# Low parts of weight units in a two-layer trunk: an accumulating DMA in place of a VectorE subtraction

## The chip, the cores and the metric

The kernel runs on one core of a Trainium2 chip. The metric is the device time of one execution in microseconds; the time before is a median of three runs, 1868.06 us (1867.34 to 1868.14). PE is TensorE, DVE is VectorE, ACT is ScalarE, POOL is GpSimd, SP is SyncE, which issues the loads.

## What is computed

Two layers on a sequence of 512 tokens of width 1024, in float32. Each layer is a feed-forward, a mixer (windowed attention beside retention) and a second feed-forward, each followed by a layer norm. Cut to what matters:

```python
D_FF = 2816
def swiglu_ffn(x, w_gu, w_down):
    a, u = jnp.split(x @ w_gu, 2, axis=-1)
    return (jax.nn.silu(a) * u) @ w_down

for l in range(2):
    x = layer_norm(ALPHA * x + 0.5 * swiglu_ffn(x, ffn1_w_gu[l], ffn1_w_down[l]), ...)
    x = layer_norm(ALPHA * x + hybrid_mixer(x, w_in[l], w_out[l], ...), ...)
    x = layer_norm(ALPHA * x + 0.5 * swiglu_ffn(x, ffn2_w_gu[l], ffn2_w_down[l]), ...)
```

## The kernel before

Every large product is made of three products in a reduced-precision form of float32: each operand is split into a high part (the value rounded, by a cast on ACT) and a low part (the value minus the high part, by a subtraction on DVE). The method split (lines 151 to 156) does that, and mm3 (158 to 163) multiplies high by high, high by low and low by high into one PSUM bank. The lines 161, 162 and 163 of the profile are these three; nearly all of PE's work has them.

The weights come as a stream of units. A unit is 128 x 1024 values as a high tile uh and a low tile ul. The class Weights holds the units in the order of their use: load brings 1 MB from HBM into one of two raw buffers (enough for two units, or for the blocks of several), then a function called cut makes the unit from it. A unit lives in one of six pairs of slots (UBUFS); pump makes the next unit as soon as done has given one back, so the cast of a unit waits for PE's last product with the unit six places before it. A raw buffer is given back when the last cut has read it.

A feed-forward has two stages.

- The up stage makes 22 chunks of the hidden layer. Its first two pairs of chunks are made by plain products, the other nine pairs by Winograd's seven products of blocks (seven_items makes the units, seven and glu7 use them). For such a pair the stream has seven units: first (the blocks A11 | A12), s12 and s34 (sums S1 | S2 and S3 | S4 of the blocks, added on DVE into a tile S), last (A22 of the gate and of the up half), and again first, s12, s34 for the up half. Units of s12 are the first ones multiplied with the sums of the input, Th and Tl; first has xh and xl. S has two buffers.
- The down stage goes over the 22 chunks of the hidden layer: rows_item makes one unit of 128 rows of w_down for each chunk, and each unit meets eight products of three matmuls. The chunk itself is split on ACT and DVE into hh and hl (line 565). The units of the last four chunks (TAIL) have slots of their own, so pools is set for them. The norm follows: norm, lines 386 to 410, on DVE with one power on POOL, and then PE's transposes (line 370) of the normed rows back into xh and xl.

The mixer's output projection takes its eight units from rows_item as well: the first four, with heads set, into mixer buffers, the last four into the common slots. Line 872 is the power on POOL in the retention, line 401 that of the norm.

The order on each engine comes from a scheduler that fills the engines' queues ahead of time; each engine then takes its queue in order, waiting on semaphores.

Of the kernel before, what the change touches and what calls it, by code (L numbers as in the profile page):

```python
# [7 lines left out]
F32 = mybir.dt.float32  # L8
# [31 lines left out]
class Weights:  # L40
    """Units of weights in the order of their use: loaded, then split into hi + lo, ahead of it."""

# [28 lines left out]
    def take(self):  # L71
        """A pair of the slots of units for something else, until done()."""
        self.out += 1
        return self.T.units()
# [6 lines left out]
    def done(self, n=1):  # L81
        self.out -= n
        self.pump()


class Trunk:
# [20 lines left out]

    # The products run as one stream; whatever hangs on other engines' results is a task that
    # yields for a number of steps of that stream.
    def spawn(self, gen, delay=0):  # L110
# [40 lines left out]
    def split(self, hi, lo, src):  # L151
        a = self.nc.scalar.copy(hi, src)  # L152
        b = self.nc.vector.tensor_sub(lo, src, hi.bitcast(F32))  # L153
        if self.pin:
            self.tc.keep_in_program_order(a)
            self.tc.keep_in_program_order(b)

    def mm3(self, out, a, b, start, stop):
        (ah, al), (bh, bl) = a, b
        mm = self.nc.tensor.matmul  # L160
        mm(out, ah, bh, start=start, stop=False)  # L161
        mm(out, ah, bl, start=False, stop=False)  # L162
        mm(out, al, bh, start=False, stop=stop)  # L163
# [5 lines left out]

# [1 line left out]
    def cols_item(self, w, c0, key):  # L171
        """Two units of 128 columns each, all rows."""
        def load():
            v = self.raw().rearrange("p (k c) -> p k c", k=KC)
            src = w[:, c0 : c0 + 256].rearrange("(k p) c -> p k c", p=P)
            if self.later is not None:
                self.later.append(lambda: self.nc.sync.dma_start(v[:, :, P:], src[:, :, P:]))
                self.nc.sync.dma_start(v[:, :, :P], src[:, :, :P])
            else:
                self.nc.sync.dma_start(v, src)  # L180
            return v

        def cut(c):
            def go(v, hi, lo):
                hv, lv = (t.rearrange("p (k c) -> p k c", k=KC) for t in (hi, lo))
                self.split(hv, lv, v[:, :, c * P : (c + 1) * P])
                return hv, lv
            return go

        return [(key, load, None, cut(c)) for c in range(2)]  # L190

    def pair_item(self, w, c0, key):
        """The same, with the columns of each head sorted into even and odd ones."""
        load = self.cols_item(w, c0, key)[0][1]
# [12 lines left out]
    def heads_item(self, w, cp, key):  # L207
        """Query heads: unit c holds head c and head 4 + c."""
        def load():
# [15 lines left out]
    def wide_item(self, w, c0, kh, key):  # L225
        """Two units of two row chunks each, 512 columns."""
        def load():
# [13 lines left out]
    def rows_item(self, w, r0, key, pools, heads=False):  # L241
        """Two units of 128 rows each, all 1024 columns; with heads, in the order of the query units."""
        def load():
# [10 lines left out]
        def cut(c):  # L254
            def go(v, hi, lo):
                self.split(hi, lo, v[:, c, :])
                return hi, lo
            return go
# [3 lines left out]
    def seven_items(self, a, u):  # L262
        """Units for the seven-product form of two pairs of column chunks: the blocks of the weights
        A11 | A12, the sums S1 | S2 and S3 | S4 of each pair, and A22 of both."""
        sums = {}
# [13 lines left out]
        def s12(q):  # L279
            def go(v, hi, lo):  # L280
                s = sums[q] = self.gpool.tile([P, 4, KC // 2, P], F32, tag="S", name=self.nm("S"), bufs=2)
                a11, a12, a21, a22 = blocks(v)
                self.nc.vector.tensor_add(s[:, 0], a21, a22)
                self.nc.vector.tensor_sub(s[:, 1], s[:, 0], a11)
                hv, lv = wide(hi), wide(lo)
                self.split(hv, lv, s[:, 0:2].rearrange("p s k c -> p (s k) c"))
                return hv, lv
            return go
# [52 lines left out]

# [1 line left out]
    def proj(self, out, u, t0, t1):  # L343
# [20 lines left out]
    def to_xT(self, src, t, c0, dst=None):  # L364
        """Transposes four 128-column chunks of token group t and splits them."""
        nc = self.nc
# [44 lines left out]

# [1 line left out]
    def tail_units(self):  # L413
        return self.units(self.fpool, "tl", TAIL)

    def ffn(self, g, b, out=None):
        nc, tc, W = self.nc, self.tc, self.W
        with ExitStack() as ctx:
# [8 lines left out]
            def sums_of_x():  # L427
                """T1 = B12 - B11, T2 = B22 - T1, T3 = B22 - B12 and -T4 = B21 - T2, split."""
                x = hT[:, NF - KC :, :]
# [26 lines left out]
            def seven(u0, getu, q, u22):  # L456
                """Winograd's form: seven products of blocks for a pair of chunks."""
                w, x, y, z = (self.ps() for _ in range(4))
# [136 lines left out]

# [1 line left out]
    def big(self, shape, dt=F32):  # L597
# [310 lines left out]
def tables():  # L908
    """Constants of the shapes alone: rotations, masks and decays."""
    import numpy as np  # L910
# [55 lines left out]
```

## Time and profile before

| | |
|---|---|
| runs, median of three | 1868.06 us (1867.34 to 1868.14) |
| profiled execution, first to last instruction (span) | 1864.8 us |
| what the runs' median has beyond that span | 3.3 us |
| granted PE clock over the span | 0.999 |
| PE, weight loads on PE, DVE, ACT, POOL busy | 99%, 91%, 72%, 43%, 5% |
| DMA: share of the 16 engines' time in loads | 30.0% |
| loads of 1 MB, median from issue to landing | 4.7 to 5.1 us |

The profiled execution has no time of its own beside its span; the runs are timed without the profiler. In a row of groups stand the line, the engine, the operation, what it writes and reads, how many of them, busy time in all and the mean in ns, and then the idle time before them with what ended it. In the list of waits stand the waiting instruction, whom it waited for, the sum in us, how often, and the longest. In a timeline stand start and length in us.

### The profile page before, as it was taken

To read this page: it belongs to the slowest core of one execution; us is meant where nothing else is said; L and a number is where in the kernel's file an instruction comes from. 1 tells how busy PE (TensorE), PEld (TensorE's weight loads), DVE (VectorE), ACT (ScalarE), POOL (GpSimd) and SP (SyncE) were. 2 spreads that over 40 slices of the span, in tenths; PEclk is the share of its full clock that TensorE was granted. 3 is DMA by queue.
4 is the path that set the end of the run, shared out by engine and by line. 5 is a ranking of instruction groups with operands and counts; after the bars stand their busy time and mean duration, and the time that the engine had idled before them with its cause. 6 is when DMAs were issued, how large, how long until landed. Compare 5 with 4: busy or idle time off the path is not lost.

```text
span 1864.8 us, 29046 instructions
## 1 busy us (share of the span) xinstructions
PE 1848.5 (99%) x12180; PEld 1691.5 (91%) x12180; DVE 1349.2 (72%) x1861; ACT 792.7 (43%) x1212; POOL 88.1 (5%) x80
## 2 busy tenths in 40 slices
PE   8999999999999999999999999999999999999998
PEld 8999988888889999998899999889888899999886
DVE  7889844657857799963688998447578577999535
ACT  5444433278622444443234444332785234444330
POOL 0000000110210000000000000002002100000001
PEclk9999999999999999999999999999999999999999
DMA  5233244122312232243212323441224122233421
GB/s 181 91 104 124 91 155 139 63 80 69 91 69 68 83 122 91 94 156 131 96 46 96 109 91 114 138 156 41 80 69 113 46 91 91 91 114 114 136 90 45
DMA packets 136930, 184.87 MB, mean 99 GB/s; under 512 B 3936, under 2 KB 115296, under 8 KB 136800
## 3 DMA queue, kind: packets, MB, share of 16 engines
q1 hardware_dynamic: 136800, 183.03, 30.0%
q8 instruction: 95, 1.56, 0.3%
q14 instruction: 35, 0.29, 0.0%
HBM read 180.92 MB, written 2.10 MB: 98 GB/s over the span
## 4 chain that ended last, share of the span: by engine, by line
PE 91%; DVE 4%; ACT 3%; DMA 1%; issue 1%; POOL 0%; POOLq 0%; SPq 0%; DVEq 0%; ACTq 0%
PE ps L161 30%; PE ps L162 29%; PE ps L163 29%; PE ps L370 1%; ACT b L785 1%; ACT sw L749 1%; DVE b L153 1%; ACT b L779 1%; DVE ul L153 1%; DMA raw<-in_w_out_dram 1%; ACT b L152 0%; DMA raw<-in_ffn_w_gu_dram 0%; DVE m L774 0%; PE ps L853 0%; PE ps L836 0%
## 5 line engine op out<-in xcount | busy, mean ns | idle before, releaser
L161 PE MATMUL ps<-xh,uh 128*128 128x256 f32 (+1 forms) x1616 | 483.2, 299 | 2.0 <-ACT uh L152 2.0
L162 PE MATMUL ps<-xl,uh 128*128 128x256 f32 (+1 forms) x1616 | 480.5, 297 | 0.0
L163 PE MATMUL ps<-xh,ul 128*128 128x256 f32 (+1 forms) x1616 | 480.2, 297 | 0.0
L153 DVE TENSOR_TENSOR ul<-raw,uh 128x1024 fp32r<-128x1024 f32 (+1 forms) x332 | 348.9, 1064 | 115.1 <-ACT uh L152 113.4
L152 ACT CAST uh<-raw 128x1024 fp32r<-128x1024 f32 (+1 forms) x332 | 298.9, 918 | 311.6 <-PE ps L162 252.1
L161 PE MATMUL ps<-Th,uh 128*128 128x256 f32 x1152 | 326.0, 283 | 0.0
L162 PE MATMUL ps<-Tl,uh 128*128 128x256 f32 x1152 | 326.0, 283 | 0.0
L163 PE MATMUL ps<-Th,ul 128*128 128x256 f32 x1152 | 326.0, 283 | 0.0
L161 PEld LDWEIGHTS ps<-xh,uh 128*128 128x128 f32 x1616 | 310.0, 192 | 11.6 <-ACT uh L152 2.7
L162 PEld LDWEIGHTS ps<-xl,uh 128*128 128x128 f32 x1616 | 310.2, 192 | 8.2 <-DVE xl L153 0.3
L163 PEld LDWEIGHTS ps<-xh,ul 128*128 128x128 f32 x1616 | 309.7, 192 | 8.5
L161 PE MATMUL ps<-uh,hh 128*128 128x512 f32 x640 | 249.5, 390 | 0.0
L163 PE MATMUL ps<-uh,hl 128*128 128x512 f32 x640 | 249.0, 389 | 0.0
L162 PE MATMUL ps<-ul,hh 128*128 128x512 f32 x640 | 249.0, 389 | 0.0
L161 PEld LDWEIGHTS ps<-Th,uh 128*128 128x128 f32 x1152 | 221.2, 192 | 0.0
L162 PEld LDWEIGHTS ps<-Tl,uh 128*128 128x128 f32 x1152 | 221.2, 192 | 0.0
L163 PEld LDWEIGHTS ps<-Th,ul 128*128 128x128 f32 x1152 | 221.2, 192 | 0.0
L152 ACT CAST uh<-S 128x1024 fp32r<-128x1024 f32 x144 | 151.2, 1050 | 129.5 <-PE ps L162 126.9
L153 DVE TENSOR_TENSOR ul<-S,uh 128x1024 fp32r<-128x1024 f32 x144 | 175.6, 1219 | 16.3 <-ACT uh L152 15.9
L153 DVE TENSOR_TENSOR hl<-hT,hh 128x512 fp32r<-128x512 f32 x80 | 54.3, 691 | 179.9 <-ACT hh L152 179.9
L152 ACT CAST hh<-hT 128x512 fp32r<-128x512 f32 x80 | 48.6, 622 | 223.6 <-PE ps L162 211.3
L163 PEld LDWEIGHTS ps<-uh,hl 128*128 128x128 f32 x640 | 120.1, 188 | 25.0
(137 smaller groups left out, 2389.3 us busy)
## 6 DMA issues: line engine op xcount, KB each, us to landing
raw<-in_ffn_w_gu_dram SPq DMA_DIRECT2D x86, 1024.0 KB, 5.0
raw<-in_ffn_w_down_dram SPq DMA_DIRECT2D x44, 1024.0 KB, 4.7
raw<-in_w_in_dram SPq DMA_DIRECT2D x18, 1024.0 KB, 5.1
raw<-in_w_in_dram SPq DMA_DIRECT2D x8, 512.0 KB, 4.6
raw<-in_w_out_dram SPq DMA_DIRECT2D x8, 512.0 KB, 5.7
raw<-in_w_out_dram SPq DMA_DIRECT2D x4, 1024.0 KB, 4.7
ln<-in_ln_g_dram SPq DMA_DIRECT2D x6, 512.0 KB, 3.7
ln<-in_ln_b_dram SPq DMA_DIRECT2D x6, 512.0 KB, 5.2
```

The source lines that it names most:

```text
L152: a = self.nc.scalar.copy(hi, src)
L153: b = self.nc.vector.tensor_sub(lo, src, hi.bitcast(F32))
L161: mm(out, ah, bh, start=start, stop=False)
L162: mm(out, ah, bl, start=False, stop=False)
L163: mm(out, al, bh, start=False, stop=stop)
L370: nc.tensor.transpose(b[:, c * P : (c + 1) * P], src[:, c * P : (c + 1) * P], self.ident)
L749: nc.scalar.copy(sw[q * 32 : q * 32 + 32, :n], src[o * 32 : o * 32 + 32, :n])
L779: nc.scalar.activation(s[:, cc, :nk], s[:, cc, :nk], AF.Exp, bias=m[:, cc : cc + 1], scale=SCALE, accum_out=den[:, cc : cc + 1])
L785: nc.scalar.activation(s[:, cc, :nk], s[:, cc, :nk], AF.Copy, scale=den[:, cc : cc + 1])
```

## The change

A new method split_dma makes high and low part without DVE: ACT casts the high part as before, ACT multiplies it by -1 into the low part's tile, and POOL issues a DMA that adds the source onto that tile in place (SBUF to SBUF, 128 x 1024 float32, 512 KB). It takes the place of split in s12 and, in rows_item, for every unit that has neither heads nor a pool of its own: in a feed-forward 18 units of s12 and 18 of the down stage. By the same rule it also takes the last four units of each output projection. The remaining hunks take out comments and docstrings, which moves line numbers by 4 or 5.

```diff
+    def split_dma(self, hi, lo, src):
+        self.nc.scalar.copy(hi, src)
+        self.nc.scalar.mul(lo, hi.bitcast(F32), -1.0)
+        self.nc.gpsimd.dma_start(lo.bitcast(F32), src, accum_op=ALU.add)
...
         def cut(c):
             def go(v, hi, lo):
-                self.split(hi, lo, v[:, c, :])
+                (self.split if heads or pools[0] else self.split_dma)(hi, lo, v[:, c, :])
                 return hi, lo
...
                 self.nc.vector.tensor_add(s[:, 0], a21, a22)
                 self.nc.vector.tensor_sub(s[:, 1], s[:, 0], a11)
-                hv, lv = wide(hi), wide(lo)
-                self.split(hv, lv, s[:, 0:2].rearrange("p s k c -> p (s k) c"))
-                return hv, lv
+                self.split_dma(hi, lo, s[:, 0:2].rearrange("p s k c -> p (s k c)"))
+                return wide(hi), wide(lo)
```

The order of PE's instructions is the same before and after. Three places show how the others move. First ACT in the up stage, one period of seven units in the first feed-forward; S is the tile of block sums, p and C belong to the sums of the products. Before:

```order
L152 CAST uh_1562<-S_1564 128x1024
L465 COPY p_205_1575<-ps_1570 128x256
L152 CAST uh_1602<-S_1564 128x1024
L152 CAST uh_1632<-raw_1516 128x1024
L152 CAST uh_1664<-S_1666 128x1024
L465 COPY p_220_1691<-ps_1686 128x256
L490 ACTIVATE C_1574<-C_1574 128x1024
L152 CAST uh_1718<-S_1666 128x1024
```

The same place with the change:

```order
L159 CAST uh_1571<-S_1573 128x1024
L160 ACTIVATE ul_1572<-uh_1571 128x1024
L469 COPY p_205_1585<-ps_1580 128x256
L152 CAST uh_1612<-S_1573 128x1024
L152 CAST uh_1642<-raw_1525 128x1024
L159 CAST uh_1674<-S_1676 128x1024
L160 ACTIVATE ul_1675<-uh_1674 128x1024
L494 ACTIVATE C_1584<-C_1584 128x1024
L469 COPY p_220_1702<-ps_1697 128x256
L152 CAST uh_1729<-S_1676 128x1024
```

Behind each cast of an s12 unit there is now the multiplication into ul, and the copy of the second p has changed places with the activation of C.

Second SP's queue where the down stage begins; ln is the norm's weights. Before:

```order
L251 DMA raw_2468<-in_ffn_w_down_dram 128x2x1024
L251 DMA raw_2618<-in_ffn_w_down_dram 128x2x1024
L251 DMA raw_2699<-in_ffn_w_down_dram 128x2x1024
L251 DMA raw_2749<-in_ffn_w_down_dram 128x2x1024
L382 DMA ln_3000<-in_ln_g_dram 128x1024
L383 DMA ln_3000<-in_ln_b_dram 128x1024
L251 DMA raw_2828<-in_ffn_w_down_dram 128x2x1024
```

With the change:

```order
L256 DMA raw_2485<-in_ffn_w_down_dram 128x2x1024
L256 DMA raw_2637<-in_ffn_w_down_dram 128x2x1024
L256 DMA raw_2720<-in_ffn_w_down_dram 128x2x1024
L386 DMA ln_3031<-in_ln_g_dram 128x1024
L387 DMA ln_3031<-in_ln_b_dram 128x1024
L256 DMA raw_2772<-in_ffn_w_down_dram 128x2x1024
L256 DMA raw_2853<-in_ffn_w_down_dram 128x2x1024
```

The fourth load of w_down has gone behind the two loads of the norm's weights, and from the third on a load waits for the DMAs that read the raw buffer it fills.

Third the output projection of the first mixer, on POOL and ACT. On POOL (sw is the rotation of retention, gvar the power in retention, rs that of the norm) before:

```order
L751 TENSOR_TENSOR sw_5013<-sw_5013,retS_4052 128x512
L751 TENSOR_TENSOR sw_5071<-sw_5071,retS_4052 128x512
L872 TENSOR_TENSOR gvar_5183<-gvar_5183,mhalf 128x8
L872 TENSOR_TENSOR gvar_5243<-gvar_5243,mhalf 128x8
L401 TENSOR_TENSOR rs_5391<-ve_5389,mhalf 128x1
```

With the change:

```order
L755 TENSOR_TENSOR sw_5049<-sw_5049,retS_4088 128x512
L755 TENSOR_TENSOR sw_5107<-sw_5107,retS_4088 128x512
L161 DMA ul_5126<-raw_5119 128x1024
L161 DMA ul_5330<-raw_5119 128x1024
L876 TENSOR_TENSOR gvar_5220<-gvar_5220,mhalf 128x8
L876 TENSOR_TENSOR gvar_5280<-gvar_5280,mhalf 128x8
L161 DMA ul_5343<-raw_5130 128x1024
L161 DMA ul_5350<-raw_5130 128x1024
L405 TENSOR_TENSOR rs_5431<-ve_5429,mhalf 128x1
```

The four DMAs of the projection's last units stand two by two before and behind the last two powers of retention. On ACT, where the last two of these units and the first ones of the next feed-forward are cast, before:

```order
L152 CAST uh_5304<-raw_5093 128x1024
L152 CAST uh_5310<-raw_5093 128x1024
L152 CAST uh_5314<-raw_5308 128x1024
L709 ACTIVATE rr_5290<-ps_5265 128x512
L152 CAST xh<-ps_5297 128x4x128
```

With the change:

```order
L159 CAST uh_5342<-raw_5130 128x1024
L160 ACTIVATE ul_5343<-uh_5342 128x1024
L159 CAST uh_5349<-raw_5130 128x1024
L152 CAST uh_5354<-raw_5347 128x1024
L160 ACTIVATE ul_5350<-uh_5349 128x1024
L713 ACTIVATE rr_5327<-ps_5302 128x512
L152 CAST xh<-ps_5335 128x4x128
```

The second multiplication comes behind the cast of the next feed-forward's first unit, and the activation and the cast of xh behind it.

## The prediction

> **What bounds the kernel now.** I read the page's first and fourth parts, then what TensorE (PE) waits for, then one period of the feed-forward's main stage in windows, then the casts (ACT) against the products that use them.
>
> ```profile
> span 1864.8 us, 29046 instructions
> PE 1848.5 (99%) x12180; PEld 1691.5 (91%) x12180; DVE 1349.2 (72%) x1861; ACT 792.7 (43%) x1212; POOL 88.1 (5%) x80
> PE 91%; DVE 4%; ACT 3%; DMA 1%; issue 1%; POOL 0%; POOLq 0%; SPq 0%; DVEq 0%; ACTq 0%
> ```
>
> A busy PE need not be a PE at its peak, so the waits decide. This is all of them:
>
> ```profile
> PE ps L370 <- DMA Y<-in_x_dram: 4.2, 1, 4.2
> PE ps L161 <- ACT uh L152: 2.0, 2, 1.6
> PE ps L836 <- DVE rr L829: 1.5, 4, 0.5
> PE ps L161 <- issue: 0.3, 2, 0.2
> ```
>
> Of 1864.8 us PE waits 8.0. The first two rows belong to the start of the program, which the change doesn't touch. Only the third, 1.5 us in the mixers' retention, waits for VectorE (DVE), and that is the ceiling of what a relieved DVE can give. The window of one period of the seven-product stage (columns: length, then busy time and count of PE, PEld, DVE, ACT, POOL, then clock, DMA share, GB/s) shows the same from near:
>
> ```profile
> core 0: us, PE busy (x) PEld busy (x) DVE busy (x) ACT busy (x) POOL busy (x), PEclk, DMA share, GB/s
> 138.36:158.52 20.16, 20.16 (x171) 20.16 (x170) 18.58 (x26) 9.15 (x12) 0.00 (x0) 1.00 0.32 106
> ```
>
> DVE is at 92% there and still PE never rests. So the question is not what the subtraction costs, but whether the longer way to a low part still ends before PE wants it.
>
> **The change part by part.** The subtractions that go, and the nearest rows for the ScalarE (ACT) instruction that comes:
>
> ```profile
> L153 DVE TENSOR_TENSOR ul<-raw,uh 128x1024 fp32r<-128x1024 f32 x228 | 277.8, 1223 | 112.6 <-ACT uh L152 110.9 <-PE ps L162 1.2
> L153 DVE TENSOR_TENSOR ul<-S,uh 128x1024 fp32r<-128x1024 f32 x144 | 175.6, 1219 | 16.3 <-ACT uh L152 15.9
> L152 ACT CAST uh<-S 128x1024 fp32r<-128x1024 f32 x144 | 151.2, 1050 | 129.5 <-PE ps L162 126.9 <-DVE ul L153 1.0
> L490 ACT ACTIVATE C<-C 128x1024 f32<-128x1024 f32 x36 | 38.3, 1064 | 7.6 <-DVE C L485 7.6
> ```
>
> The rule in rows_item also catches the last four units of each output projection, so 4 x 36 + 2 x 4 = 152 units change. DVE loses 152 x 1.22 = 185 us. ACT gains 152 multiplications by -1; no such row exists, a whole-tile ACTIVATE takes 1.06 us, so 161 us and ACT goes from 43% to 51%. Both lie beside PE. In a period of the main stage DVE falls to 18.58 - 2 x 1.22 = 16.1 us and ACT rises to 9.15 + 2.1 = 11.3, of 20.16. On ACT the copy of p stands behind the multiplication and slips by half a microsecond; the next cast (142.67) is not reached by it.
>
> The new step is the accumulating DMA. Call D the time from the end of ACT's multiplication to the landing. The trace has no accumulating DMA and none issued by GpSimd (POOL). The nearest rows are SyncE's (SP) loads, issue to landing, and POOL's own small operation:
>
> ```profile
> raw<-in_ffn_w_gu_dram SPq DMA_DIRECT2D x86, 1024.0 KB, 5.0
> raw<-in_ffn_w_down_dram SPq DMA_DIRECT2D x44, 1024.0 KB, 4.7
> raw<-in_w_in_dram SPq DMA_DIRECT2D x8, 512.0 KB, 4.6
> L401 POOL TENSOR_TENSOR rs<-ve,mhalf 128x1 f32<-128x1 f32 x24 | 35.8, 1490 | 1490.2 <-DVE ve L399 1490.2
> ```
>
> Low end: 4.6 us, as a plain 512 KB load. High end: two reads and a write of 512 KB one after the other, 3 x 4.6 = 13.8. The value I take: the accumulation reads 1 MB in all, so 5.0, plus 1.5 for POOL's share (its cheapest row): D = 6.5. It lies near the low end because 512 KB more cost a load only 0.4 us. DMA is busy a third of the time (0.32 above), so meeting a load may add a third of 5.0, 1.6 us: D = 8.1.
>
> Now what D may be. In the main stage, ACT's casts and the products that first use the unit:
>
> ```profile
> 139.74 1.05 ACT L152 CAST uh<-S 128x1024 fp32r<-128x1024 f32 x1 [0.34 <-PE ps L162]
> 142.67 1.05 ACT L152 CAST uh<-S 128x1024 fp32r<-128x1024 f32 x1 [0.99 <-PE ps L162]
> 148.43 1.05 ACT L152 CAST uh<-S 128x1024 fp32r<-128x1024 f32 x1 [1.83 <-PE ps L162]
> ...
> 152.50 0.28 PE L163 MATMUL ps<-xh,ul 128*128 128x256 f32 x1
> 152.62 0.28 PE L161 MATMUL ps<-Th,uh 128*128 128x256 f32 x1
> 152.86 0.28 PE L163 MATMUL ps<-Th,ul 128*128 128x256 f32 x1
> ...
> 162.94 0.28 PE L163 MATMUL ps<-Th,ul 128*128 128x256 f32 x1
> ```
>
> A cast starts when a slot of the six comes free, so its lead is fixed by PE's pace. PE turns from xh to Th where an S1|S2 unit begins; the low part is first read at 152.86. 152.86 - 139.74 - 1.05 - 1.06 leaves 11.0 us for D. The pair's other unit: 162.94 - 148.43 - 2.11 = 12.4. Above 11.0 each of the 36 pairs stalls PE by the excess (the stall then covers the second unit).
>
> The start of the down products is tighter:
>
> ```profile
> 229.02 1.05 ACT L152 CAST uh<-raw 128x1024 fp32r<-128x1024 f32 x1 [1.78 <-PE ps L162]
> 233.40 1.05 ACT L152 CAST uh<-raw 128x1024 fp32r<-128x1024 f32 x1
> ...
> 240.70 0.40 PE L162 MATMUL ps<-ul,uh 128*128 128x512 f32 x1
> ...
> 262.48 0.39 PE L162 MATMUL ps<-ul,hh 128*128 128x512 f32 x1
> ```
>
> The first unit leaves 240.70 - 229.02 - 2.11 = 9.6 us. The fifth needs a raw buffer that the first two units' DMAs must first release, where the subtractions did: the second's multiplication ends at 235.51, then D, a load of 4.7, cast, a cast of hh between, and multiplication (2.7), and D again before 262.48. 2D <= 19.5, so D <= 9.8. SP's queue is moved there: the loads of the norm's weights now stand ahead of the fourth raw load. They wait for DVE and PE as before, so this costs nothing unless D passes the same bounds.
>
> The output projection is tightest:
>
> ```profile
> 533.70 1.06 ACT L152 CAST uh<-raw 128x1024 fp32r<-128x1024 f32 x1 [0.76 <-PE ps L163]
> 535.06 1.06 ACT L152 CAST uh<-raw 128x1024 fp32r<-128x1024 f32 x1 [0.30 <-PE ps L163]
> 536.42 1.06 ACT L152 CAST uh<-raw 128x1024 fp32r<-128x1024 f32 x1 [0.30 <-PE ps L163]
> ...
> 548.34 0.39 PE L162 MATMUL ps<-ul,xh 128*128 128x512 f32 x1
> ...
> 548.99 1.36 DVE L393 SCALAR_TENSOR_TENSOR Y<-Y,ps 128x512 f32<-128x512 f32 x2 [4.17 <-PE ps L163]
> 553.63 1.28 DVE L405 SCALAR_TENSOR_TENSOR Y<-Y,rs,ln 128x1024 f32<-128x1024 f32 x1 [0.45 <-POOL rs L401]
> ...
> 560.88 0.38 PE L370 MATMUL ps<-ident,Y 128*128 128x128 f32 x2
> ```
>
> These are the projection's last two units and the first of the next feed-forward. With the two multiplications among them, five instructions in a row, the last multiplication ends at 533.70 + 5 x 1.06 = 539.0, and its unit is read at 548.34: D <= 9.3. Its raw buffer takes the next feed-forward's second load. DVE's subtraction for that load stands ahead of the norm in DVE's queue, so the norm now waits for 539.0 + D, a load (5.0), cast (1.06) and subtraction (1.22): 546.3 + D. The norm takes 554.91 - 548.99 = 5.9 us and PE transposes its result at 560.9, so the subtraction may end at 555.0: D <= 8.7.
>
> On POOL two of the four DMAs of this projection stand ahead of the last two powers of retention, two behind them. The second unit's cast and the first of those powers:
>
> ```profile
> 508.08 1.06 ACT L152 CAST uh<-raw 128x1024 fp32r<-128x1024 f32 x1
> 521.44 1.64 POOL L872 TENSOR_TENSOR gvar<-gvar,mhalf 128x8 f32<-128x8 f32 x1 [11.86 <-DVE gvar L871]
> ```
>
> The multiplication ends near 510.2, eleven microseconds before the power, so POOL is free again by then. Behind the other waits stand: on ACT the casts of hh behind a cast whose raw buffer lands late, on SP the norm's weights and later loads behind a load whose buffer a DMA still reads. Both recur at the end of the down products; that place is not priced here and counts under the first rival below.
>
> The sum at D = 6.5 to 8.1: every new wait is covered, by PE's own products of the units in between. The cover is gone at 8.7. The gain is between 0 and the 1.5 us of L836; the output projection's subtractions stand near two of those four waits, so I take 0.6. Profiled span 1864.8 - 0.6; the runs' median lies 1868.06 - 1864.8 = 3.3 us above the span, for what lies around it. Forecast: 1868.06 - 0.6, about 1867.5, within 0.2% (3.7 us, about what a measurement of this kernel can tell from no change).
>
> **The rivals.** *The DMA is a little slow* (D from 8.7 to 11.0): the main stage still hides it. At 11.0 the down products lose 11.0 - 9.6 = 1.4 for the first unit and 2 x 11.0 - 19.5 - 1.4 = 1.1 for the fifth, x 4 = 10 us, the projections (11.0 - 9.3) x 2 = 3: up to about 1881. For it: meeting loads; against: 8.1 already has one.
>
> *The DMA is slow* (D over 11.0), slower than before: the place is the S1|S2 units, the price 36 us for each microsecond over 11.0. At 13.8: 36 x 2.8 = 101, down 4 x (4.2 + 3.9) = 32, projections 2 x 4.5 = 9, together 142: 2010. For it: nothing in the trace shows how fast a DMA adds; against: the loads' rows.
>
> [...]
>
> *DVE's relief shows elsewhere*: a gain over 3.7 us would need more than the 1.5 us of waits that DVE causes; nothing speaks for it. That the change does less than it says can be left out, since it even reaches 8 units more.
>
> **How the numbers follow.** Hidden: 0.62. A little slow: 0.14, of which 0.02 stays within 0.2%. Slow: 0.16. Descriptors held up: 0.05. Faster by over 0.2%: 0.03. So faster 0.03, same 0.64, slower 0.33. The range reaches up through the second case and into the third as far as D = 11.4 (0.4 x 36 = 14, down 4 x 3.3 = 13, projections 4: 1899), and down to the edge of the faster case; left out are 0.14, 0.03 and 0.02. So 1864 to 1900.
>
> **What would show it.** Right: PE's waits for uh, ul and DMA stay as they are, the DMAs land under 8.7 us after the multiplication, a main-stage period stays 20.16 with DVE near 16.1 and ACT near 11.3, L836 waits less than 1.5. [...]

## The result, and the profile with the change

The changed kernel takes 1888.35 us (median of 4 runs, 1884.20 to 1893.73); the kernel before took 1867.70 beside it (4 runs, 1866.94 to 1868.14). The ratio is 1.0112, 95% interval 1.0100 to 1.0125: 20.7 us slower. The forecast was 1867.5, no change that can be measured, in a range from 1864 to 1900.

The page of the profiled execution with the change (1889.85 us by the clock, its span in the first row):

```profile
span 1887.7 us, 29464 instructions
PE 1858.9 (98%) x12180; PEld 1694.7 (90%) x12180; DVE 1175.2 (62%) x1709; ACT 940.1 (50%) x1364; POOL 220.3 (12%) x232
q1 hardware_dynamic: 136800, 183.03, 30.6%
q0 software_dynamic: 21888, 79.70, 22.3%
```

The engines moved as costed. DVE fell by 174 us (185 forecast), ACT rose by 147 (161 forecast; the rows overlap the next one by some 0.1 us), and the additions take 22.3% of the 16 DMA engines' time, 2.8 us of all sixteen for each of the 152. Yet the span grew by 22.9 us, from 1864.8 to 1887.7. PE is busy 10.4 us longer than the 1848.5 before, and it waits longer. All its waits with the change:

```profile
PE ps L166 <- ACT hh L152: 9.1, 4, 3.8
PE ps L374 <- DMA Y<-in_x_dram: 4.3, 1, 4.3
PE ps L168 <- DVE hl L153: 3.6, 6, 0.8
PE ps L166 <- ACT uh L152: 1.6, 1, 1.6
PE ps L840 <- DVE rr L833: 0.6, 2, 0.3
PE ps L166 <- issue: 0.3, 2, 0.2
PE ps L167 <- DVE xl L153: 0.3, 1, 0.3
```

That is 19.8 us against 8.0, 11.8 more; with the 10.4 it makes 22.2 of the 22.9. New are the rows for hh and hl, the split hidden values of the down products, and 0.3 us for xl. No row names a DMA into ul; a low part that lands too late is what the prediction's rivals of a slow and of a little slow DMA priced.

The up stage lost nothing. One period of it (columns as in the prediction):

```profile
138.40:158.60 20.20, 20.20 (x170) 20.20 (x170) 16.54 (x23) 11.17 (x14) 1.72 (x2) 1.00 0.59 156
```

DVE 16.5 and ACT 11.2 were forecast as 16.1 and 11.3, and PE never rests. A single addition there, from ACT's multiplication through POOL's issue to the landing:

```profile
140.47 1.06 ACT L160 ACTIVATE ul<-uh 128x1024 fp32r<-128x1024 f32 x1
```

```profile
141.93 0.86 POOL L161 DMA_DIRECT2D ul<-S  x1 [10.64 <-ACT p L469]
```

```profile
ul<-S POOLq DMA_DIRECT2D x2, 512.0 KB, 5.4
```

The multiplication ends at 141.53, the issue starts 0.4 us later and the landing comes 5.4 after that: D = 5.8, under the 6.5 that was taken for an addition alone.

The loss sits at the end of the down products of the first three feed-forwards; the fourth has no stage behind it. Set against the same instructions before, PE falls behind by 9.5 us between 334 and 351, by 10.1 between 922 and 935 and by 4.5 between 1282 and 1290. ACT at the first of these places:

```profile
312.06 1.05 ACT L159 CAST uh<-raw 128x1024 fp32r<-128x1024 f32 x1 [5.66 <-DMA raw<-in_ffn_w_down_dram]
313.14 1.06 ACT L160 ACTIVATE ul<-uh 128x1024 fp32r<-128x1024 f32 x1
314.10 0.60 ACT L152 CAST hh<-hT 128x512 fp32r<-128x512 f32 x1
314.61 1.05 ACT L159 CAST uh<-raw 128x1024 fp32r<-128x1024 f32 x1
322.67 1.05 ACT L152 CAST uh<-raw 128x1024 fp32r<-128x1024 f32 x1 [7.01 <-DMA raw<-in_ffn_w_down_dram]
323.63 1.06 ACT L160 ACTIVATE ul<-uh 128x1024 fp32r<-128x1024 f32 x1
...
332.82 1.04 ACT L152 CAST uh<-raw 128x1024 fp32r<-128x1024 f32 x1 [6.68 <-DMA raw<-in_ffn_w_down_dram]
333.77 0.61 ACT L152 CAST hh<-hT 128x512 fp32r<-128x512 f32 x1
...
342.72 1.04 ACT L152 CAST uh<-raw 128x1024 fp32r<-128x1024 f32 x1 [4.44 <-DMA raw<-in_w_in_dram]
343.67 0.61 ACT L152 CAST hh<-hT 128x512 fp32r<-128x512 f32 x1
```

The weight casts wait in brackets for loads, and behind each stands a cast of hh that needs nothing from that load: PE stops for the hh at 333.77 and again for the one at 343.67. The weights are not what PE lacks; they are cast many products ahead. It lacks the hh that queues behind them on ACT.

Why are the loads late? This is when SP issued the load of the last pair of down units, and behind it the next stage's first load. Before:

```profile
305.85 0.37 SPq L251 DMA_DIRECT2D raw<-in_ffn_w_down_dram  x1
308.60 0.37 SPq L180 DMA_DIRECT2D raw<-in_w_in_dram  x1
```

With the change, 21 us later, while PE was not late at all by then:

```profile
326.90 0.37 SPq L256 DMA_DIRECT2D raw<-in_ffn_w_down_dram  x1
330.07 0.37 SPq L185 DMA_DIRECT2D raw<-in_w_in_dram  x1
```

And this is how long the stage's DMAs took from issue to landing. Before:

```profile
raw<-in_ffn_w_down_dram SPq DMA_DIRECT2D x8, 1024.0 KB, 4.7
```

With the change, the median loads and additions of the stage, and the one addition that SP's load of 304.05 waited for:

```profile
raw<-in_ffn_w_down_dram SPq DMA_DIRECT2D x9, 1024.0 KB, 7.7
ul<-raw POOLq DMA_DIRECT2D x15, 512.0 KB, 6.8
...
ul<-raw POOLq DMA_DIRECT2D x1, 512.0 KB, 9.4
```

A raw buffer now goes round like this: load 7.7, cast, multiplication, cast of hh, cast, multiplication, 4.7 (the ACT rows from 312.06 to 314.61, the cast's 1.05 and a multiplication of 1.06), 0.4 to the issue, addition 6.8 to 9.4. That is 19.6 to 22.2 us for a pair of units. PE uses up a pair in 2 x 5.44 = 10.9 us (from 240.70 to 262.48, four units, in the prediction's rows), and with two buffers a round may last 21.8. Before, a round held load 4.7 and some 4 us of casts and subtractions. These are SP's loads of the stage; a load goes to the same buffer as the one two rows above it, so the time between the two is a round:

| load of pair | before | with the change | later by | round before | round with the change |
|---|---|---|---|---|---|
| 3 | 235.73 | 240.87 | 5.1 | | |
| 4 | 241.49 | 251.44 | 10.0 | | |
| 5 | 248.87 | 261.51 | 12.6 | 13.1 | 20.6 |
| 6 | 254.82 | 270.23 | 15.4 | 13.3 | 18.8 |
| 7 | 265.08 | 281.63 | 16.6 | 16.2 | 20.1 |
| 8 | 275.96 | 292.32 | 16.4 | 21.1 | 22.1 |
| 9 | 286.84 | 304.05 | 17.2 | 21.8 | 22.4 |
| 10 | 297.72 | 315.20 | 17.5 | 21.8 | 22.9 |
| 11 | 305.85 | 326.90 | 21.1 | 19.0 | 22.9 |

Before, the first rounds are far shorter than 21.8 and build a lead over PE. With the change they are nearly as long as PE's use, so 15 of the 21 us are there by the sixth load: the third load took 9.5 us and an addition beside it 10.0, while the loads of the norm's weights, too, ran beside them. The last four rounds, 22.1 to 22.9 us, lie a little over 21.8, so nothing is won back.

Nearly half of the loss is the clock. The windows around the second wait of that place:

```profile
340.70:344.10 3.40, 1.03 (x5) 0.53 (x3) 0.30 (x1) 1.38 (x2) 0.00 (x0) 1.00 1.21 290
344.10:347.50 3.40, 2.96 (x6) 1.42 (x6) 3.40 (x5) 2.94 (x5) 0.00 (x0) 0.50 0.42 99
347.50:350.90 3.40, 3.29 (x7) 2.15 (x8) 3.37 (x5) 1.22 (x2) 0.00 (x0) 0.50 0.87 286
350.90:354.30 3.40, 3.40 (x16) 2.80 (x16) 1.70 (x3) 0.00 (x0) 0.00 (x0) 1.00 0.91 291
```

PE rested 2.4 us of the first window; in the next two its granted clock is 0.50 and it makes 13 matmuls; in the last one, at full clock, it makes 16. There are three such stretches at 0.5 that the trace before has not, of 6.8, 10.2 and 3.4 us, one behind each of the three places: 20.5 us at half speed, 10.2 lost, the 10.4 by which PE's busy time grew.

### The profile page after: what moved, and what is told of

Same layout as the page of the kernel before. It is cut to its first block, busy times and chain, and to the rows that moved or that the text cites. A ratio compares the mean times of both kernels' runs of the same rounds, so it can differ in the third digit from the quotient of the medians.

```text
span 1887.7 us, 29464 instructions
## 1 busy us (share of the span) xinstructions
PE 1858.9 (98%) x12180; PEld 1694.7 (90%) x12180; DVE 1175.2 (62%) x1709; ACT 940.1 (50%) x1364; POOL 220.3 (12%) x232
## 3 DMA queue, kind: packets, MB, share of 16 engines
q0 software_dynamic: 21888, 79.70, 22.3%
## 4 chain that ended last, share of the span: by engine, by line
PE 57%; DMA 8%; issue 6%; ACT 4%; DVE 4%; POOL 1%; POOLq 0%; SPq 0%; DVEq 0%; ACTq 0%
PE ps L166 18%; PE ps L168 18%; PE ps L167 18%; DMA raw<-in_ffn_w_down_dram 4%; DMA ul<-raw 3%; PE ps L374 1%; ACT b L789 1%; DVE ul L153 1%; DMA raw<-in_w_in_dram 1%; ACT b L783 1%; ACT sw L753 1%; ACT uh L152 1%; POOL ul L161 1%; DMA raw<-in_ffn_w_gu_dram 1%; PE ps L857 0%
## 5 line engine op out<-in xcount | busy, mean ns | idle before, releaser
L152 ACT CAST uh<-raw 128x1024 fp32r<-128x1024 f32 (+1 forms) x252 | 215.3, 877 | 322.0 <-PE ps L167 214.4
L153 DVE TENSOR_TENSOR ul<-raw,uh 128x1024 fp32r<-128x1024 f32 (+1 forms) x252 | 251.5, 1013 | 128.7 <-ACT uh L152 128.3
L166 PEld LDWEIGHTS ps<-xh,uh 128*128 128x128 f32 x1616 | 309.9, 192 | 11.4 <-ACT uh L152 2.5
L168 PE MATMUL ps<-uh,hl 128*128 128x512 f32 x640 | 252.8, 395 | 4.1 <-DVE hl L153 3.6
L159 ACT CAST uh<-raw 128x1024 fp32r<-128x1024 f32 x80 | 83.3, 1047 | 167.5 <-DMA raw<-in_ffn_w_down_dram 146.7
L160 ACT ACTIVATE ul<-uh 128x1024 fp32r<-128x1024 f32 x152 | 160.7, 1060 | 4.2
L166 PEld LDWEIGHTS ps<-uh,hh 128*128 128x128 f32 x640 | 121.7, 190 | 35.8 <-ACT hh L152 11.0
L161 POOL DMA_DIRECT2D ul<-S x72 | 62.7, 871 | 778.5 <-ACT p L469 414.6
```

The source lines that it names most:

```text
L160: self.nc.scalar.mul(lo, hi.bitcast(F32), -1.0)
L161: self.nc.gpsimd.dma_start(lo.bitcast(F32), src, accum_op=ALU.add)
```

## The experiments

Theory A says that the loss is made in the down products alone. There are five candidates for what makes it there:

- A1, the longer round of the two raw buffers;
- A2, the full DMA engines as such;
- A3, the queue on ACT;
- A4, the additions' traffic and their holding of the buffer together;
- A5, one unlucky place on ACT (the multiplication at 323.63 above, which stands behind a cast that waits 7 us).

Ratios are to the kernel before, run beside each.

### Each half alone

Sums alone: `split_dma` stays in s12, rows_item goes back to `self.split(hi, lo, v[:, c, :])`. Rows alone: rows_item keeps the change, s12 goes back.

> The accumulating DMA is kept for the S1|S2 units alone (72 of the 152); the down units and the last output-projection units go back to the VectorE subtraction. Theory A (the loss is made in the down products, where loads and accumulating DMAs share two raw buffers and the DMA engines): no loss left, 1866 to 1869 us, a ratio within 0.998 to 1.001, PE waits as before, no clock of 0.5 after 15 us. Rival B (each accumulating DMA costs a little everywhere, on the engines or the memory): about half of the 20.7 us stays, 1877 to 1879.

> The other half: the accumulating DMA for the down units and the last output-projection units alone (80 of 152), the S1|S2 units split by VectorE as before. Theory A: the whole loss, 1884 to 1894 us (ratio 1.009 to 1.013), with PE waiting for hh and hl at the end of three of the four feed-forwards. Rival B: about half, 1877 to 1879.

Sums alone: 1867.20 us, ratio 1.0002 (0.9992 to 1.0011). Rows alone: 1888.77, ratio 1.0113 (1.0096 to 1.0130). So theory A holds: the 72 additions of the up stage cost nothing, though the DMA share of that stage is 0.60 in this run too, and the other 80 cost it all. The waits of rows alone are those of the whole change (for hh 9.1 us in 4 places, for hl 3.4 in 5).

### Traffic without holding, holding without traffic

To the kernel before, rows_item adds something behind `self.split` of each of the 72 down units; dst is space that is dead in that stage, and nobody waits for it. Of each edit the line that does it is shown.

```diff
# idle additions, from the high part
+    self.nc.gpsimd.dma_start(dst, hi.bitcast(F32), accum_op=ALU.add)
# idle additions, from the raw buffer
+    self.nc.gpsimd.dma_start(dst, v[:, c, :], accum_op=ALU.add)
# holding by POOL
+    for _ in range(1 + 2 * c):
+        self.nc.gpsimd.tensor_tensor(out=dst, in0=v[:, c, :], in1=v[:, c, :], op=ALU.add)
```

> The kernel before, with an accumulating DMA of the same size for each of the 72 down units that nobody waits for: it reads the high part, not the raw buffer, and writes into space that is dead in that stage (the first few of each feed-forward into one place, one after the other). It adds the DMA work without the chain. Theory A4 (the loss needs both: loads and additions slow each other to 8 to 10 us, and each addition stands in the chain load, cast, multiplication, addition, release of one of two raw buffers): the loads lengthen from 4.7 to 7 or more, yet load plus cast plus subtraction, some 14 us for two pairs of units of 21.8 us of products, keep up: 1866 to 1871 us. Theory A2 (full DMA engines alone): the loads come late as in the changed kernel, 1880 to 1890.

> The kernel before, with GpSimd reading each down unit's raw data again (one addition of 128x1024 into dead space for the first unit of a pair, three for the second, an estimated 2.6 us each from the 1.3 us of 128x512): the raw buffers are held some 10 us longer, as by the accumulating DMA, without a byte of DMA. Theory A4: load 4.7 plus a hold of 13 stays under 21.8 us for two pairs: 1866 to 1871 us. Theory A1 (the holding alone): 1880 to 1890, with late loads and PE waiting for hh.

> The kernel before, with an accumulating DMA for each of the 72 down units that nobody waits for, as in the run of idle additions, except that it reads the raw buffer: the buffer is held until it lands. ScalarE has no multiplication and its order is that of the kernel before. Theory A4 (addition work and holding together make the loss, wherever the low part comes from): 1880 to 1890 us, though either alone cost 2 and 10. If the multiplications and their order on ScalarE are what counts: 1868 to 1876.

Idle additions from the high part: 1869.83, ratio 1.0012 (1.0002 to 1.0022). From the raw buffer: 1868.30, ratio 1.0007 (0.9998 to 1.0017). The down stage from 250 to 316, first with the change, then with each of the two (the same columns as above):

```profile
250.00:316.00 66.00, 66.00 (x293) 54.66 (x292) 7.62 (x11) 32.97 (x38) 11.32 (x13) 1.00 0.86 202
```

```profile
250.00:316.00 66.00, 66.00 (x293) 54.68 (x292) 23.83 (x25) 19.74 (x24) 13.06 (x15) 1.00 0.93 233
```

```profile
250.00:316.00 66.00, 66.00 (x293) 54.66 (x292) 23.11 (x25) 19.34 (x24) 12.22 (x14) 1.00 0.98 249
```

The DMA engines are fuller (0.93 and 0.98 against 0.86) and 2 us or less are lost, not 21. A2 falls. A4 as it was put falls too: in the last run an addition holds the raw buffer until it lands, and yet the loss is 1 us and not 20. What that run lacks is the row of steps: after the first few of a stage, its additions start as soon as the load has landed, two at a time and beside the casts, and not behind cast and multiplication. Its loads are late as well in the middle of the stage, by some 15 us (264.40 for 248.87 at the fifth pair, 280.24 for 265.08 at the seventh). But its rounds from the fifth load on take 13.6 to 18.7 us, under PE's 21.8, so they win it back: the last two loads go out at 312.49 and 314.65, six to seven us later than before, not 21.

The run with POOL took 1877.82, ratio 1.0053 (1.0035 to 1.0071), and tells less than it should: DVE's subtraction for hl, 691 ns before, took two and a half times as long in the mean of the run (2.31 us for the 52 of 80 that met an addition of POOL's, 0.68 for the others),

```profile
L154 DVE TENSOR_TENSOR hl<-hT,hh 128x512 fp32r<-128x512 f32 x80 | 138.3, 1743 | 11.4 <-ACT hh L153 11.4
```

so DVE itself was late there, and the 10 us can't be put down to the holding. The time lies between the two forecasts.

### Which link of the round

Third buffer: in the down products, the loads of the 4th, 7th and 10th pair go to a buffer from the stage's own pool (the expectation names two of them; the condition below holds for the 4th as well). Last pair: the ninth pair's two units, the last that change in a down stage, go back to DVE. Ninth only: of the down units these two alone have the change, and s12 keeps it. Of each edit the lines that matter are shown.

```diff
# third buffer, in rows_item's load
+    third = self.fx is not None and (r0 // 256) % 3 == 0
+    v = self.raw(third).rearrange("p (c n) -> p c n", c=2)
# last pair
-    (self.split if heads or pools[0] else self.split_dma)(hi, lo, v[:, c, :])
+    (self.split if heads or pools[0] or r0 // 256 == (NF - TAIL) // 2 - 1 else self.split_dma)(hi, lo, v[:, c, :])
```

> As the changed kernel, with a third raw buffer during the down products (for the loads of the 7th and 10th pair of units). Theory A1 (two raw buffers held longer: each load waits for the release of an accumulating DMA, so load, cast, multiplication and addition stand in one chain): the chain is loosened and most of the loss goes, 1867 to 1873 us. Theory A2 (the 16 DMA engines themselves are full in that stage: one more buffer moves no more bytes): 1882 to 1892, with the late loads still late.

> The changed kernel with the two units of the ninth pair of each down stage (8 units of 152) split by VectorE again; they are the ones whose second multiplication stands behind the next pair's waiting cast. Theory A5 (that one late release): half of the loss goes or more, 1870 to 1879 us. If the lateness has been built up over the whole stage: 1881 to 1889.

> The S1|S2 units and only the ninth pair of each down stage (72 + 8 units) by accumulating DMA, all else by VectorE. Theory A1 with a lead (the first pairs eat the lead, the ninth only presents the bill): the loads are as in the kernel before up to the last pair, the last two come less than 10 us later, and PE waits no more than 2 us: 1866 to 1870 us. If those 8 units cost by themselves what undoing them gave back: 1880 to 1887.

Last pair back: 1870.15, ratio 1.0017 (1.0008 to 1.0026): undoing 8 units of 152 gives back 18 of the 21 us, and the time lies at the lower edge of what was expected under A5. Ninth alone: 1868.45, ratio 1.0006 (0.9996 to 1.0016), as expected under A1: by themselves these units cost nothing, so A5 can't be the whole cause. Together that is a lead that earlier pairs eat and a last link that presents the bill. SP's last two loads with the last pair back (the first row holds the tenth and the eleventh pair's, 0.5 us apart), and with the ninth alone:

```profile
317.70 0.88 SPq L256 DMA_DIRECT2D raw<-in_ffn_w_down_dram  x2
325.94 0.37 SPq L185 DMA_DIRECT2D raw<-in_w_in_dram  x1
```

```profile
307.81 0.37 SPq L256 DMA_DIRECT2D raw<-in_ffn_w_down_dram  x1
315.30 0.37 SPq L185 DMA_DIRECT2D raw<-in_w_in_dram  x1
```

In the first the tenth load is 20 us late (17.5 with the change), but the ninth pair's buffer comes free without an addition, and the eleventh load goes out 8.7 us earlier than the 326.90 above. In the second nothing was late ahead of them, and the two go out 2 and 7 us later than before.

The third buffer alone: 1889.47, ratio 1.0114 (1.0099 to 1.0129), no help, which speaks against A1. Its trace says why. ACT there (L163 is the cast of a changed unit, L156 that of a last-four unit or of hh):

```profile
310.48 1.05 ACT L156 CAST uh<-raw 128x1024 fp32r<-128x1024 f32 x1 [12.40 <-DMA raw<-in_ffn_w_down_dram]
...
313.85 1.05 ACT L163 CAST uh<-raw 128x1024 fp32r<-128x1024 f32 x1
...
316.41 1.04 ACT L163 CAST uh<-raw 128x1024 fp32r<-128x1024 f32 x1
324.43 1.05 ACT L156 CAST uh<-raw 128x1024 fp32r<-128x1024 f32 x1 [6.98 <-DMA raw<-in_ffn_w_down_dram]
```

With the third buffer the scheduler put the tenth pair's cast ahead of the ninth's. ACT stood 12.4 us for the tenth's load while the ninth pair, loaded first, waited behind. What the buffer had won (6.7 us at the eighth pair's cast, 297.03 against 303.75) was lost again.

### ACT's queue

Of each edit the lines that matter are shown, with ... between distant ones; in the second, "chain" keeps an instruction behind the one given.

```diff
# hh early: two more chunks split ahead, six buffers of hh and hl
-            ahead = [next(split), next(split)]
+            ahead = [next(split) for _ in range(4)]
# multiplication first: each cast is made to follow the last multiplication, in split
-        a = self.nc.scalar.copy(hi, src)
+        a = self.chain(self.nc.scalar.copy(hi, src), self.mul)
# and in split_dma
-        self.nc.scalar.copy(hi, src)
-        self.nc.scalar.mul(lo, hi.bitcast(F32), -1.0)
+        self.chain(self.nc.scalar.copy(hi, src), self.mul)
+        self.mul = self.nc.scalar.mul(lo, hi.bitcast(F32), -1.0)
# hh far: chunks 2 to 17 go to xh and xl, which are dead in this stage
+                        hh, hl = self.xh[:, f % KC, :], self.xl[:, f % KC, :]
...
-            ahead = [next(split), next(split)]
+            ahead = [next(split) for _ in range(8)]
# negated first
+        self.nc.scalar.mul(lo, src, -1.0)
+        self.nc.gpsimd.dma_start(lo.bitcast(F32), src, accum_op=ALU.add)
         self.nc.scalar.copy(hi, src)
-        self.nc.scalar.mul(lo, hi.bitcast(F32), -1.0)
-        self.nc.gpsimd.dma_start(lo.bitcast(F32), src, accum_op=ALU.add)
```

> As the changed kernel, with the splits of the hidden values (hh, hl) made two units further ahead (six buffers in place of four). Theory A3 (PE waits only because the casts of hh stand behind casts of uh on ScalarE whose raw load is late, while the weight units themselves have a lead of up to six): the stalls go although the loads stay late, 1867 to 1873 us. If the weight units themselves come too late (A2 in its strong form), PE waits for uh or ul in place of hh and the time stays at 1882 to 1892.

> The changed kernel with one thing pinned: ScalarE multiplies right behind its own cast, no other weight cast stands between. In the changed kernel the last multiplication of each down stage stands behind the next pair's cast, which waits 7 us for a load, so its addition and the release of its raw buffer come 8 us late. Theory A5 (that order makes a good part of the late loads at the end): 1874 to 1882 us. If it only shifts who waits: 1885 to 1892.

> The changed kernel with the hidden values split eight units ahead (into the space of xh and xl, which is dead in the down products; the last four as before), so that no cast of hh stands behind a late weight cast. Theory A3 (PE's loss is all waits for hh, the weight units themselves are in time): 1867 to 1872 us. If the weight units are late as well, PE waits for uh, ul or the next stage's first values in their place: 1874 to 1886.

> The changed kernel with ScalarE's two instructions exchanged: it writes the negated rounded value straight from the raw data, the addition is issued, and the cast to the high part follows. The same DMA work and the same two raw buffers, but each addition starts one ScalarE instruction (1.06 us) earlier and no longer stands behind the next pair's cast. Theory A1 (the length of the chain through a raw buffer): the last loads of a down stage come 3 to 8 us earlier, 1872 to 1883 us. If only the DMA's own time counts: 1885 to 1891.

Hh two further ahead: 1880.65, ratio 1.0072 (1.0057 to 1.0087), 8 us less than with the change and between the two forecasts, although the loads go out as late as ever (325.98 and 329.12). So the queue on ACT makes part of it. Hh eight ahead: 1889.55, ratio 1.0119 (1.0103 to 1.0135), longer than either forecast. In this kernel the split of the chunk eight further on is written over the one that the products still had to read, so a chunk's products take that later one and wait for it; still it shows that the waits don't go away when hh is out of the queue:

```profile
PE ps L167 <- DVE xl L153: 8.5, 4, 3.0
PE ps L374 <- DVE Y L409: 5.1, 4, 2.0
```

No row for hh is left; PE waits for the norm and the next stage's first xl in its place, behind DVE's subtractions for the same late weights. A3 is not the whole: late loads find the next queue.

Multiplication first was to prove A5 and went the other way: 1901.31, ratio 1.0185 (1.0168 to 1.0202). Tying the casts to the multiplications also moved the casts of hh, of which three had stood in a row ahead of the stage's third pair:

```profile
250.93 1.05 ACT L160 CAST uh<-raw 128x1024 fp32r<-128x1024 f32 x1 [9.74 <-DMA raw<-in_ffn_w_down_dram]
...
252.97 0.60 ACT L153 CAST hh<-hT 128x512 fp32r<-128x512 f32 x1
```

Now the first hh stands behind the third pair's late cast, and PE waits 21.8 us for hh in 11 places, from the start of the stage on. So it doesn't test A5; it shows what the order on ACT is worth with late loads: 13 us more than with the change, though no new work came in. Negated first also took longer than either forecast: 1896.37, ratio 1.0171 (1.0130 to 1.0212). The last down load did go out 7 us earlier (319.95 for 326.90), the next stage's did not (329.92), and the time got worse. The scheduler again changed the places of hh among the waiting casts (PE waits 11.8 us for them in 6 places). How much the earlier loads gave and the new order took stays open.

### Buffers and queue together

Three cures at once: third buffer, multiplication first, hh far with seven chunks ahead. Two of them: the same without the third buffer.

> The changed kernel with three things at once: a third raw buffer for two of the loads of each down stage, ScalarE's multiplication right behind its cast, and the hidden values split seven units ahead (in xh and xl, dead in that stage), so that a late load holds back no cast of hh. Theory A1 with A5 (a chain through two raw buffers and an unlucky order on ScalarE): the loss goes, 1867 to 1873 us. Theory A2 (full DMA engines): loads stay late and PE waits for them in some other place, 1880 to 1890.

> The same with two raw buffers: multiplication right behind its cast, hidden values split seven units ahead. If the two raw buffers are the bound, the next stage's weights still come late: 1876 to 1888 us, against 1867 to 1873 with the third buffer. If ScalarE's order was the cause, this one too lies at 1867 to 1873.

Three: 1873.11, ratio 1.0035 (1.0022 to 1.0048), at the edge of what A1 with A5 forecast. Two: 1878.62, ratio 1.0062 (1.0045 to 1.0079), in the range that was forecast if the two raw buffers are the bound. The last two loads with two buffers:

```profile
325.30 0.37 SPq L257 DMA_DIRECT2D raw<-in_ffn_w_down_dram  x1
326.75 0.37 SPq L186 DMA_DIRECT2D raw<-in_w_in_dram  x1
```

and with three:

```profile
310.64 0.37 SPq L262 DMA_DIRECT2D raw<-in_ffn_w_down_dram  x1
321.26 0.37 SPq L190 DMA_DIRECT2D raw<-in_w_in_dram  x1
```

With the order on ACT held fast, the third buffer brings the last load 15 us forward, and at the ends of its down stages PE has no wait left in that run: its new waits are 4.6 us for hh at the starts of stages (2.7 us of them at 251.4), where the cure itself put the first hh behind a waiting cast. With two buffers PE still waits 6.6 us behind the second down stage, for Y and xl. In time the third buffer is worth 5.5 us here, with intervals that just overlap. So A1 holds, where the third buffer alone had seemed to refute it. And A5 is not enough: with two buffers the ninth pair's second addition was issued at 316.2, nine us earlier than the 325.09 with the change, yet the next load went out at 325.30, because that addition, beside a load, took 9.0 us. The late multiplication is the last link of a late round, not the cause of it.

No version beat the kernel before; the one with the sums alone equals it. PE never waited for DVE in the up stage, so there is nothing there to gain.

## Why the prediction was wrong, point by point

- *D = 6.5 alone.* Right in kind, a little high: 5.8 in the up stage. That an addition takes little longer than a load of 512 KB (5.4 us from issue to landing against the 4.6 of the prediction's row) was read from the right rows.
- *D = 8.1 where it meets loads.* Too low where it counted. The estimate took the DMA share of the up stage before (0.32). In the down stage with the change the share is 0.86, loads take 7.7 in place of 4.7, and additions 6.8 in the median and up to 9.4 or 10.0, past the 8.7 at which the text said the cover was gone.
- *The bounds on D.* The up stage's 11.0 and 12.4 held: no loss. The out-projection's 8.7 to 9.3 held: PE has no wait there. The first down unit's 9.6 and the fifth's 9.8 held in the sense that PE never waits for a low part. The bounds were on the wrong thing: they asked when PE reads ul, and PE is not delayed by ul. It came close once: the ninth pair's second low part landed at 330.0, some 3 us before the products that read it.
- *The step that failed* is the sentence "Both recur at the end of the down products; that place is not priced here and counts under the first rival". It named the mechanism, casts of hh behind a cast whose raw buffer lands late, and left it without a price. The fifth unit's bound, 2D for one round of a buffer, was taken once, at the start of the stage; it should have been taken as a rate: load + two casts and multiplications + D against 21.8 us for two pairs, over 11 pairs. With 7.7 + 4.7 + 0.4 + 9.4 = 22.2 that has no slack, and the last four rounds measured 22.1 to 22.9. Two terms of that bound were too small as well: the load at the start of the stage took 9.5 us where 4.7 was put, and the addition beside it 10.0 where D was 8.1. In place of the covered waits of the forecast, PE waits 12.7 us for hh and hl at the ends of the down stages.
- *The cover "by PE's own products of the units in between"* is a stock, and the forecast treated it as if every unit had its own. By the last load of the stage the change had used up 21 us of it, and the casts of hh had none left.
- *The rivals.* "A little slow" named other places in the down products, the first and the fifth unit, and its price (up to 1881) fell short of the 1888. The range reached as far as 1888 through another mechanism, waits for ul at D up to 11.4; that the measured time lies in it is luck. "Slow" didn't happen: no wait for ul appeared. The 0.05 for descriptors held up, long issues on POOL beside a busy DVE, is a term that no run shows: of the 72 issues of POOL's in the up stage, the 58 that fell nearly whole into busy time of DVE took 0.87 us each, as long as the 5 that met next to none of it.
- *The gain at L836*, 0.6 us forecast, was 0.9 (1.5 to 0.6).
- *The clock* was in no term. Nearly half of the loss comes from it, 10.2 of 22.9 us.

What stays open is how much of the loss each of the two, late loads and the order on ACT, would make by itself, since every edit to one moved the other, and how much the norm's weight loads beside the first additions add to the early lateness, since no run moved them alone. Shown is that the loss needs the longer round: 18 of the 21 us go when the last pair is undone, and with the order on ACT held a third buffer takes away the waits at the ends of the down stages. Shown is also that the late loads reach PE through the casts in ACT's queue.

## What to carry to other kernels

When a step takes longer to give back a buffer, price the whole round of that buffer (load, casts, the step, each as long as it gets beside the other transfers) against what the consumer uses per buffer, over the whole stage; a lead hides the difference until it is used up, and the bill comes at the far end, in the queue that happens to stand behind the late load. Nothing is gained by relieving a busy engine that nobody waits for (DVE at 92% here). Undo a change at its last link as well as in halves: without 8 units of 152 nearly all of the loss was gone, and by themselves these 8 cost nothing.

## What the runs showed of the hardware

- After 1.4 to 2.4 us of rest of PE within 3.4 us the granted clock was 0.5 for 3.4, 6.8 or 10.2 us, and 11.8 us of new waits became 22.9 us of span. With the change these stretches start at 344.09, 924.35 and 1286.17 and last 6.83, 10.24 and 3.41 us; their starts are 170 and 106 times the length of the shortest, 3.413 us, apart. In that trace the 3.41 us just before them hold 2.36, 1.88 and 1.43 us of rest; two others, from 330.44 and from 333.85, hold 1.05 and 1.19 and were not followed by 0.5. No run shows how much rest it takes: with three cures PE rested 2.66 us of the 66 from 250 to 316, in one wait of 2.7 us, and the granted clock there stayed at 1.00.
- An addition by DMA of 512 KB from SBUF to SBUF landed 5.2 us (sums) or 5.5 us (rows) after its issue (medians over the run with the change), hardly longer than the loads of 1 MB for the up stages in the same run (5.2), and used 2.8 us of the 16 engines (22.3% of the span over 152).
- Loads by SP and additions by POOL took longer beside each other: with the idle additions from the high part, at a DMA share of 0.93, a load took 9.5 us and an addition 7.5, 9.7 or 10.0 (medians of the first down stage, by the tile they write); with the ninth pair alone, when only two additions fell into that stage, a load took 4.8 us and an addition 4.7. The share by itself does not say how much: with those from the raw buffer, most of which start when a load has landed, it was 0.98, and loads took 5.6 us and additions 6.0, 7.2 or 8.8 (medians, by the tile they write).
- Beside POOL's additions, which read a raw buffer in SBUF, DVE's subtraction of 128x512 took 2.31 us in place of 0.69 (the 52 that met one; 0.68 for the others, 1.74 in the mean of all 80).
